# The first column pair of a feed-forward network: w1's combinations kept for the second half of the tokens

## The chip, the cores and the metric

The kernel runs on one core of a Trainium2 chip. The time is that of one execution on the device in microseconds (us); a median of three runs is given. TensorE (PE) does matmuls and transposes, VectorE (DVE) and GpSimd (POOL) do elementwise work on tiles in SBUF, ScalarE (ACT) does copies, casts and activations, and SyncE (SP) issues the DMAs. Each engine works through its own queue in order; semaphores make it wait for the others.

## What is computed

The reference is one layer of an encoder over 1024 tokens of 1024 channels. The part that matters here is the last but one line:

```python
h = _layer_norm(DEEPNORM_ALPHA * h + y @ w_out[l], ln1_g[l], ln1_b[l])
f = (jax.nn.silu(h @ ffn_w1[l]) * (h @ ffn_w3[l])) @ ffn_w2[l]
h = _layer_norm(DEEPNORM_ALPHA * h + f, ln2_g[l], ln2_b[l])
```

`ffn_w1` and `ffn_w3` are 1024 x 2816, `ffn_w2` is 2816 x 1024, all in float32.

## The kernel before

Products of float32 matrices are made of three matmuls each: every operand is split into a high part (a cast on ScalarE, L1384) and a low part (a subtraction, L1385, on POOL or on VectorE), and `mm3` (L160 to L162) adds high x high, high x low and low x high.

The feed-forward part multiplies blocks by a scheme of Strassen's kind: seven products of combined blocks in place of eight. Rows of w1 and w3 are halved over the 1024 input channels, columns over pairs of column tiles: pair p takes column tiles p and p + 11, p = 0 to 10. Tokens are halved into two *halves* h = 0, 1 of 256 columns each (a column stands for two tokens, one from each block). For each pair, w1 and then w3 give seven combined left operands, here called *pieces* 1 to 7 (`split` in `ff_stream`, tiles fc, hi and lo). The combinations are made by VectorE: L1575, L1576, L1579 and L1581. `H[h][i]` is the right operand of product i for half h. `ff_hidden` multiplies piece by piece into PSUM banks (fx, fz, fy), copies them out with ScalarE (L1633, L1639, L1642, L1644), adds on VectorE (L1636, L1645, L1648), applies silu (L1622) after w1 and multiplies by it after w3 (L1625). The four result blocks are then combined for the second matrix product (LEFT, seven left sides), split into high and low parts and written to HBM (`put_by`, tiles fg, L1658, L1385, L1661 into d_f).

All pairs but the first are done for both halves at once (512 columns). The first pair is done for half 0, then for half 1, and `ff_stream` loads, combines and splits w1 and w3 anew for the second half. Half 0 needs only the normalised tokens 512 to 1023 (`turn` 0 and 1), half 1 the rest. `turn` (L1507 to L1535) transposes two token tiles (ot on TensorE, hb copies L1519), scales and saves them (L1520, L1521, d_acc), combines them (L1528, L1529, L1532, L1535) and splits the seven combinations into H. `turn` 2 and 3 are called after `ff_stream` has been started and run beside the first products. What precedes them is the layer norm, whose last step is L1466.

Tiles live in named places (tags) that are handed round in rings: "w" raw weights (4), "s" sums (2), "c" pieces (6), "e" results (8), "g" left sides (2). A tile's new use waits until its old one is read. P0 to P5 and T5 held the token tiles (acc) before, T7, WR, WL and WH what `turn` 2 and 3 combine (hb), LA0, LA1, C1 and C2 the output weights.

The order on each engine is set by a scheduler at build time, from the order of the calls, priorities and its own estimate of times; nothing is reordered while the kernel runs.

Of the kernel before, what the change touches and what calls it, by code (L numbers as in the profile page):

```python
# [13 lines left out]
R = mybir.dt.float32r  # L14
I32 = mybir.dt.int32
AF = mybir.ActivationFunctionType
ALU = mybir.AluOpType
# [8 lines left out]
NF = FF // 128  # L26
# [113 lines left out]
class Trunk:  # L140
# [1407 lines left out]


    def ff_order(self):  # L1550
        return [(0, (0,)), (0, (1,))] + [(p, (0, 1)) for p in range(1, NF // 2)]


    def ff_stream(self):
        nc, A = self.nc, self.A
        tt = nc.vector.tensor_tensor
        self.rings = {"w": ["Z0", "Z1", "MW", "T6"], "s": ["P0", "P1"], "c": ["Z2", "P2", "LA0", "LA1", "C1", "C2"],
                      "e": ["P3", "P4", "P5", "T5", "T7", "WR", "WL", "WL"], "g": ["WH", "WH"]}
        self.banks = ["pj", "q", "fs", "q", "z", "pj", "q", "fs"]

        def split(x, eng=None):
            c = self.ring("c", [128, 2, 4, 128], R)
            self.split_to(c[:, 0], c[:, 1], x.rearrange("p (k n) -> p k n", k=4), eng)
            return c[:, 0], c[:, 1]
        for p, hs in self.ff_order():
            for nm in ("w1", "w3"):
                raw = [self.ring("w", [128, 2, 512]) for i in range(2)]
                for i in range(2):
                    nc.sync.dma_start(out=raw[i].rearrange("p a n -> p (a n)"), in_=A[nm][p + i * NF // 2])
                (a11, a12), (a21, a22) = ([x[:, i] for i in range(2)] for x in raw)  # L1570
                yield split(a11)
                yield split(a12)
                s = self.ring("s", [128, 2, 512])
                a5, a6 = s[:, 0], s[:, 1]
                tt(out=a5, in0=a21, in1=a22, op=ALU.add)  # L1575
                tt(out=a6, in0=a5, in1=a11, op=ALU.subtract)  # L1576
                yield split(a6, nc.vector)
                yield split(a5)
                tt(out=a21, in0=a11, in1=a21, op=ALU.subtract)  # L1579
                yield split(a21)  # L1580
                tt(out=a12, in0=a12, in1=a6, op=ALU.subtract)  # L1581
                yield split(a12, nc.vector)
                yield split(a22)

    def ff_next(self):
        if len(self.ahead) < 4:
# [7 lines left out]
        return x  # L1594


    def ff_hidden(self, p, hs):
        nc = self.nc
        tt = nc.vector.tensor_tensor
        n = 256 * len(hs)  # L1600
        cs = slice(256 * hs[0], 256 * hs[0] + n)


        def product(i, ps, first):
            hi, lo = self.ff_next()
            for a, h in enumerate(hs):
                x = self.H[h][i]
                for k in range(4):
                    self.mm3(ps[:, 256 * a:256 * a + 256], hi[:, k], lo[:, k], x[:, 0, :, k], x[:, 1, :, k],
                             first and a == 0 and k == 0, a == len(hs) - 1 and k == 3, True)  # L1610
        act = [None] * 4
        have, put = {}, set()
        for w in range(2):
            ea, eb = (self.ring("e", [128, 2, 512])[:, :, :n] for i in range(2))
            e1, e2, e3, e5 = ea[:, 0], ea[:, 1], eb[:, 0], eb[:, 1]
            if w == 0:
                ex = self.ring("e", [128, 2, 512])[:, :, :n]


            def done(i, dst, src):  # L1620
                if w == 0:
                    nc.scalar.activation(out=dst, in_=src, func=AF.Silu)  # L1622
                    act[i] = dst
                else:
                    tt(out=dst, in0=src, in1=act[i], op=ALU.mult)  # L1625
                    have[i] = dst
                    for m, (a, *b) in enumerate(LEFT):
                        if m not in put and all(j in have for j in (a, *b[:1])):
                            put.add(m)
                            self.put_by(m, p, cs, have[a], *((have[b[0]], b[1]) if b else ()))  # L1630
# [6 lines left out]
            done(0, e1, e1)  # L1637
# [8 lines left out]
            done(3, e3, e3)  # L1646
            product(5, y, False)
            tt(out=e2, in0=y, in1=e2, op=ALU.add)  # L1648
            done(1, e2, e2)
            product(6, x, False)  # L1650
            done(2, ex[:, w], x)


    def put_by(self, m, p, cs, x, y=None, op=None):
        nc = self.nc
        g = self.ring("g", [128, 2, 512])[:, :, :cs.stop - cs.start]
        if y is not None:
            nc.vector.tensor_tensor(out=g[:, 1], in0=x, in1=y, op=op)  # L1658
            x = g[:, 1]
        self.split_to(g[:, 0].bitcast(R), g[:, 1], x, nc.vector)  # L1660
        nc.sync.dma_start(out=self.d_f[m, p, :, :, cs], in_=g)  # L1661

# [160 lines left out]
            nc.sync.dma_start(out=out, in_=o)  # L1823

    def ffn(self):
        for p, hs in self.ff_order():
            self.ff_hidden(p, hs)
        self.ff_second()


# [11 lines left out]
```

## Time and profile before

| | us |
|---|---|
| median of 3 runs (lowest, highest) | 1462.27 (1462.12, 1463.15) |
| profiled execution, its own time | 1465.01 |
| its span, first to last instruction | 1462.2 |
| TensorE matmul busy | 1323.2 (90%) |
| VectorE busy | 1100.0 (75%) |
| ScalarE busy | 621.7 (43%) |
| POOL busy | 575.7 (39%) |
| mean granted clock of TensorE | 0.958 |

Times within the profile count from the start of the span. The feed-forward part begins at 774.65 us; its second product begins at about 1230 us. Matmuls are pipelined: one of 128x256 is listed with 0.28 us but the next starts some 0.12 us later, so progress is read from the starts, and "busy" is the time covered. A row of a timeline gives start, duration, engine, line, operation and tiles (out<-in), the count, and in brackets the idle time of the engine before it and what ended it. The granted clock is 1.00 at 2.4 GHz and 0.50 at 1.2 GHz.

### The profile page before, as it was taken

What the parts mean: (1) busy time and instruction counts of PE and PEld (TensorE: products, weight loads), DVE (VectorE), ACT (ScalarE), POOL (GpSimd) and SP (SyncE); (2) the same over time, 40 slices, a digit from 0 to 9 for tenths busy, and PEclk for the clock granted to TensorE, in tenths of its full rate; (3) what the DMA queues carried; (4) which work ended last, traced back from release to release, by engine and by line L of the source; (5) the groups of instructions that cost most, each with busy time, mean ns of one, the idle gap of its engine ahead of it and who ended that gap; (6) DMA issues with size and microseconds to landing.
All of it is one profiled execution on the core that took longest, in us unless ns stands there. A gap on an engine that the chain in (4) does not pass through costs nothing.

```text
span 1462.2 us, 23749 instructions
## 1 busy us (share of the span) xinstructions
PE 1323.2 (90%) x9072; PEld 1196.4 (82%) x9072; DVE 1100.0 (75%) x1910; ACT 621.7 (43%) x1205; POOL 575.7 (39%) x524
## 2 busy tenths in 40 slices
PE   6968797977797999999877899999999999999997
PEld 5968787766796787877766899999999999888885
DVE  8997966487997685779999866666676665346888
ACT  4312141656324785761426544444444444332231
POOL 6466663153574332325567633333333331000006
PEclk9989998999899898999999899999999999999999
DMA  6111033122325004244312434444444438996752
GB/s 241 49 54 29 13 94 87 44 70 89 87 73 180 2 15 148 84 128 154 118 70 87 138 123 159 147 147 143 157 147 142 150 137 291 385 315 234 273 188 115
DMA packets 97056, 193.95 MB, mean 133 GB/s; under 512 B 24624, under 2 KB 50864, under 8 KB 96944
## 3 DMA queue, kind: packets, MB, share of 16 engines
q1 hardware_dynamic: 94912, 187.59, 38.3%
q10 hardware_dynamic: 2032, 4.86, 1.0%
q8 instruction: 71, 1.16, 0.3%
q14 instruction: 41, 0.34, 0.1%
HBM read 127.41 MB, written 63.96 MB: 131 GB/s over the span
## 4 chain that ended last, share of the span: by engine, by line
PE 42%; DVE 12%; DMA 3%; issue 2%; ACT 1%; POOL 1%; DVEq 0%; SPq 0%; ACTq 0%; POOLq 0%
PE fx L160 5%; PE fx L162 5%; PE fx L161 5%; PE f L160 4%; PE f L162 4%; PE f L161 4%; PE fy L162 2%; PE fy L160 2%; PE fy L161 2%; DVE acc L1435 1%; PE fz L160 1%; PE fz L161 1%; PE fz L162 1%; DMA fw<-w 1%; PE ops L161 1%
## 5 line engine op out<-in xcount | busy, mean ns | idle before, releaser
L160 PE MATMUL proj<-HA,wh 128*128 128x256 f32 x672 | 195.5, 291 | 14.6 <-DVE la L919 11.8
L160 PE MATMUL fx<-H,fc 128*128 128x256 f32 x704 | 196.9, 284 | 5.7 <-ACT fc L1384 2.2
L161 PE MATMUL proj<-HB,wh 128*128 128x256 f32 x672 | 200.1, 298 | 1.7 <-POOL HB L334 1.7
L162 PE MATMUL proj<-HA,wl 128*128 128x256 f32 x672 | 196.6, 293 | 4.1 <-POOL wl L394 4.1
L162 PE MATMUL fx<-H,fc 128*128 128x256 f32 x704 | 197.8, 282 | 2.6 <-DVE fc L1385 2.6
L1385 POOL TENSOR_TENSOR fc<-fw,fc 128x512 fp32r<-128x512 f32 x96 | 137.3, 1432 | 158.5 <-ACT fc L1384 157.7
L161 PE MATMUL fx<-H,fc 128*128 128x256 f32 x704 | 198.5, 282 | 0.0
L160 PEld LDWEIGHTS proj<-HA,wh 128*128 128x128 f32 x672 | 131.8, 196 | 18.4 <-issue 7.7
L162 PEld LDWEIGHTS proj<-HA,wl 128*128 128x128 f32 x672 | 131.5, 196 | 10.0 <-issue 5.5
L160 PEld LDWEIGHTS fx<-H,fc 128*128 128x128 f32 x704 | 132.5, 190 | 7.8 <-ACT fe L1633 2.7
L161 PEld LDWEIGHTS proj<-HB,wh 128*128 128x128 f32 x672 | 131.5, 196 | 7.0 <-issue 4.8
L162 PEld LDWEIGHTS fx<-H,fc 128*128 128x128 f32 x704 | 133.7, 191 | 2.8 <-DVE fc L1385 2.8
L161 PEld LDWEIGHTS fx<-H,fc 128*128 128x128 f32 x704 | 134.1, 191 | 0.1
L160 PE MATMUL f<-fb,fa 128*128 128x512 f32 x276 | 108.9, 395 | 0.0
L162 PE MATMUL f<-fb,fa 128*128 128x512 f32 x276 | 108.9, 394 | 0.0
L161 PE MATMUL f<-fb,fa 128*128 128x512 f32 x276 | 108.7, 394 | 0.0
L160 PE MATMUL fy<-H,fc 128*128 128x256 f32 x352 | 100.0, 284 | 4.7 <-ACT fe L1642 3.6
L162 PE MATMUL fy<-H,fc 128*128 128x256 f32 x352 | 99.5, 284 | 0.2 <-DVE fc L1385 0.2
L161 PE MATMUL fy<-H,fc 128*128 128x256 f32 x352 | 99.5, 283 | 0.0
L1821 POOL TENSOR_TENSOR acc<-acc,g 128x1024 f32<-128x1024 f32 x4 | 11.6, 2904 | 205.8 <-ACT acc L1820 205.8
L1384 ACT CAST fc<-fw 128x512 fp32r<-128x512 f32 x120 | 73.7, 619 | 31.8 <-POOL fc L1385 15.7
L1385 POOL TENSOR_TENSOR fc<-fs,fc 128x512 fp32r<-128x512 f32 x24 | 33.4, 1391 | 119.4 <-ACT fc L1384 116.0
(602 smaller groups left out, 3761.6 us busy)
## 6 DMA issues: line engine op xcount, KB each, us to landing
fa<-d_f SPq DMA_DIRECT2D x77, 512.0 KB, 3.8
d_f<-fg SPq DMA_DIRECT2D x70, 512.0 KB, 2.9
fw<-w SPq DMA_DIRECT2D x48, 512.0 KB, 3.6
fg<-w SPq DMA_DIRECT2D x44, 256.0 KB, 5.3
wraw<-w_in SPq DMA_DIRECT2D x16, 512.0 KB, 4.0
xt<-x SPq DMA_DIRECT2D x8, 512.0 KB, 8.1
oraw<-w_out SPq DMA_DIRECT2D x8, 512.0 KB, 3.7
yraw<-d_y SPq DMA_DIRECT2D x8, 512.0 KB, 4.1
```

What stands on the lines that cost most here:

```text
L160: mm(out, whi, xhi, start=start, stop=False, skip_group_check=shared)
L161: mm(out, whi, xlo, start=False, stop=False, skip_group_check=shared)
L162: mm(out, wlo, xhi, start=False, stop=stop, skip_group_check=shared)
L1384: nc.scalar.copy(out=hi, in_=raw)
L1385: (eng or nc.gpsimd).tensor_tensor(out=lo, in0=raw, in1=hi.bitcast(F32), op=ALU.subtract)
L1435: nc.vector.tensor_tensor(out=ht, in0=ht, in1=self.row4[1], op=ALU.add)
L1821: nc.gpsimd.tensor_tensor(out=o, in0=o, in1=self.g2, op=ALU.mult)
```

## The change

The first pair is still done by halves, but in the order w1 half 0, w3 half 0, w1 half 1, w3 half 1, all within one call of `ff_hidden`. The seven pieces of w1 made for half 0 are kept in a ring of their own ("k": Z2, P2, P3, T7, WR, WH, WH; tiles fk) and used again for half 1. w3's pieces are made twice, as before. While the first pair lasts, pieces of w3 have four places (C1, C2, LA0, LA1) and results five (P4, P5, T5, WL, WL), allocated once at full width and written by halves. The left sides are put by once, after the second half, 512 wide, into the tiles of ring "k", which the second use of w1 has then released. After that the places of "k" go to rings "c", "e" and "g".

```diff
     def ff_order(self):
-        return [(0, (0,)), (0, (1,))] + [(p, (0, 1)) for p in range(1, NF // 2)]
+        split = [(w, (h,)) for h in range(2) for w in range(2)]
+        return [split] + [[(w, (0, 1)) for w in range(2)] for p in range(1, NF // 2)]
...
-        self.rings = {"w": ["Z0", "Z1", "MW", "T6"], "s": ["P0", "P1"], "c": ["Z2", "P2", "LA0", "LA1", "C1", "C2"],
-                      "e": ["P3", "P4", "P5", "T5", "T7", "WR", "WL", "WL"], "g": ["WH", "WH"]}
+        self.rings = {"w": ["Z0", "Z1", "MW", "T6"], "s": ["P0", "P1"], "c": ["C1", "C2", "LA0", "LA1"],
+                      "e": ["P4", "P5", "T5", "WL", "WL"], "g": [], "k": ["Z2", "P2", "P3", "T7", "WR", "WH", "WH"]}
...
-            c = self.ring("c", [128, 2, 4, 128], R)
+            c = self.ring(ring, [128, 2, 4, 128], R)
...
+        for p, steps in enumerate(self.ff_order()):
+            kept = []
+            for w, hs in steps:
+                if kept and w == 0:
+                    yield from kept
+                    continue
+                ring = "c" if len(hs) == 2 or w else "k"
+                for x in parts(("w1", "w3")[w], p):
+                    if ring == "k":
+                        kept.append(x)
+                    yield x
...
+        tiles = [[self.ring("e", [128, 2, 512]) for i in range(3 - w)] for w in range(2)]
+        for w, hs in steps:
+            n = 256 * len(hs)
+            cs = slice(256 * hs[0], 256 * hs[0] + n)
...
+                tt(out=dst, in0=src, in1=act[i, hs], op=ALU.mult)
+                if hs[-1] == 1:
+                    have[i] = all_
...
+                            self.put_by(m, p, have[a], *((have[b[0]], b[1]) if b else ()))
...
+        if p == 0:
+            k = self.rings["k"]
+            self.rings["c"] += k[:2]
+            self.rings["e"] += k[2:5]
+            self.rings["g"] += k[5:]
...
+    def put_by(self, m, p, x, y=None, op=None):
         nc = self.nc
-        g = self.ring("g", [128, 2, 512])[:, :, :cs.stop - cs.start]
+        g = self.ring("g" if self.rings["g"] else "k", [128, 2, 512])
...
-        nc.sync.dma_start(out=self.d_f[m, p, :, :, cs], in_=g)
+        nc.sync.dma_start(out=self.d_f[m, p], in_=g)
```

`parts(nm, p)` is the body that loads one matrix's raw tiles and yields its seven pieces, unchanged; lines move down by one to 17 (L1575 to L1576 and so on). The scheduler puts the engines' instructions into another order. VectorE, from the end of the last layer norm on, before (fs_705 and fw_699, fw_700 are the second half's w1, fc_688 the third piece of w3, H and hb belong to `turn` 3):

```order
L1575 TENSOR_TENSOR fs_705_7266<-fw_700_7220 128x512
L1385 TENSOR_TENSOR H_654_6918<-hb_664_6970,H_654_6918 128x512
L1576 TENSOR_TENSOR fs_705_7266<-fs_705_7266,fw_699_7219 128x512
L1579 TENSOR_TENSOR fw_700_7220<-fw_699_7219,fw_700_7220 128x512
L1528 TENSOR_TENSOR hb_666_6972<-hb_664_6970 128x512
L1581 TENSOR_TENSOR fw_683_7085<-fw_683_7085,fs_687_7123 128x512
L1529 TENSOR_TENSOR hb_666_6972<-hb_665_6971,hb_666_6972 128x512
L1532 TENSOR_TENSOR hb_664_6970<-hb_665_6971,hb_664_6970 128x512
L1535 TENSOR_TENSOR hb_665_6971<-hb_665_6971,hb_666_6972 128x512
L1385 TENSOR_TENSOR H_655_6919<-hb_666_6972,H_655_6919 128x512
L1645 TENSOR_TENSOR fe_672_7020<-fe_672_7020 128x256
L1385 TENSOR_TENSOR fc_688_7126<-fs_687_7123,fc_688_7126 128x512
```

The same place now (fk_682 is piece 6 of w1, fc_695 piece 6 of w3, fz_699 product 2 of w1 for half 1):

```order
L1385 TENSOR_TENSOR H_654_6918<-hb_664_6970,H_654_6918 128x512
L1385 TENSOR_TENSOR fc_695_7181<-fw_685_7087,fc_695_7181 128x512
L1648 TENSOR_TENSOR fe_671_7019<-fz_680_7047,fe_671_7019 128x256
L1648 TENSOR_TENSOR fe_674_7022<-fz_694_7179,fe_674_7022 128x256
L1528 TENSOR_TENSOR hb_666_6972<-hb_664_6970 128x512
L1529 TENSOR_TENSOR hb_666_6972<-hb_665_6971,hb_666_6972 128x512
L1532 TENSOR_TENSOR hb_664_6970<-hb_665_6971,hb_664_6970 128x512
L1535 TENSOR_TENSOR hb_665_6971<-hb_665_6971,hb_666_6972 128x512
L1636 TENSOR_TENSOR fe_674_7022<-fe_674_7022,fe_671_7019 128x256
L1648 TENSOR_TENSOR fe_671_7019<-fz_699_7284,fe_671_7019 128x256
L1385 TENSOR_TENSOR H_655_6919<-hb_666_6972,H_655_6919 128x512
L1385 TENSOR_TENSOR fk_682_7053<-fw_645_6843,fk_682_7053 128x512
```

The three combinations of the second half's w1 are gone, the fourth combination of w3 (L1581, now L1582) and the low part of its third piece stand further up, and the low part of w1's piece 6 has come in after the turn. POOL, over the same time, before:

```order
L1385 TENSOR_TENSOR H_654_6918<-hb_665_6971,H_654_6918 128x512
L1385 TENSOR_TENSOR fc_686_7105<-fw_683_7085,fc_686_7105 128x512
L1385 TENSOR_TENSOR H_656_6920<-hb_658_6922,H_656_6920 128x512 x2
L1385 TENSOR_TENSOR fc_697_7202<-fw_684_7086,fc_697_7202 128x512
L1385 TENSOR_TENSOR fc_689_7143<-fs_687_7123,fc_689_7143 128x512
L1385 TENSOR_TENSOR H_656_6920<-hb_665_6971,H_656_6920 128x512
L1385 TENSOR_TENSOR H_654_6918<-hb_666_6972,H_654_6918 128x512
L1385 TENSOR_TENSOR H_655_6919<-hb_664_6970,H_655_6919 128x512
L1385 TENSOR_TENSOR fc_701_7223<-fw_699_7219,fc_701_7223 128x512
L1385 TENSOR_TENSOR H_656_6920<-hb_665_6971,H_656_6920 128x512
```

And POOL now (fk_679, fk_681 and fk_683 are pieces 4, 5 and 7 of w1, fc_696 is piece 7 of w3):

```order
L1385 TENSOR_TENSOR H_654_6918<-hb_665_6971,H_654_6918 128x512
L1385 TENSOR_TENSOR H_656_6920<-hb_658_6922,H_656_6920 128x512 x2
L1385 TENSOR_TENSOR fk_679_7031<-fs_677_7025,fk_679_7031 128x512
L1385 TENSOR_TENSOR H_656_6920<-hb_665_6971,H_656_6920 128x512
L1385 TENSOR_TENSOR fc_696_7198<-fw_686_7088,fc_696_7198 128x512
L1385 TENSOR_TENSOR H_654_6918<-hb_666_6972,H_654_6918 128x512
L1385 TENSOR_TENSOR H_655_6919<-hb_664_6970,H_655_6919 128x512
L1385 TENSOR_TENSOR fk_681_7049<-fw_646_6844,fk_681_7049 128x512
L1385 TENSOR_TENSOR H_656_6920<-hb_665_6971,H_656_6920 128x512
L1385 TENSOR_TENSOR fk_683_7070<-fw_646_6844,fk_683_7070 128x512
```

Low parts of w3 and of the second half's w1 have made room for those of w1's pieces 4, 5 and 7. On SyncE, the loads now (fw_715 and fw_716 are w1 of the next pair, fw_701 and fw_702 w3 of the second half):

```order
L1570 DMA fw_715_7445<-w1 128x1024
L1521 DMA d_acc_95<-acc_641_6825 128x1024
L1570 DMA fw_716_7446<-w1 128x1024
L1570 DMA fw_701_7313<-w3 128x1024
L1570 DMA fw_702_7314<-w3 128x1024
L1570 DMA fw_739_7643<-w3 128x1024
L1678 DMA d_f_96<-fk_712_7424 128x1024
```

The loads of the second half's w1 are gone, and w1 of the next pair is asked for ahead of w3 of the second half.

## Rows read from the trace of the kernel before

**Rows 1.** Stretches of the span: the stretch and its length, busy time of each engine with its count of instructions, TensorE's granted clock, the busy share of the DMA engines, GB/s.

```profile
774.65:790.00 15.35, 11.20 (x78) 10.34 (x77) 15.21 (x19) 12.60 (x23) 11.84 (x8) 0.89 0.51 172
790.00:806.07 16.07, 9.43 (x71) 8.33 (x69) 16.07 (x12) 10.46 (x21) 14.79 (x10) 0.91 0.08 33
...
860.00:880.00 20.00, 20.00 (x172) 20.00 (x171) 12.87 (x15) 8.56 (x16) 8.00 (x7) 1.00 0.27 90
880.00:900.00 20.00, 20.00 (x171) 19.99 (x170) 14.68 (x20) 10.03 (x18) 6.68 (x6) 1.00 0.60 212
```

The columns after the length are PE, PEld (weight loads), DVE, ACT and POOL.

**Rows 2.** TensorE in order of time, from the first matmul of the feed-forward part to the last wait of its start; the last row groups the transposes up to 806 us (busy time, mean ns, idle before).

```profile
774.65 0.36 PE L160 MATMUL fx<-H,fc 128*128 128x256 f32 x1
...
806.07 0.58 PE L162 MATMUL fx<-H,fc 128*128 128x256 f32 x1 [2.56 <-DVE fc L1385]
806.45 0.41 PE L160 MATMUL fx<-H,fc 128*128 128x256 f32 x1
806.66 0.41 PE L161 MATMUL fx<-H,fc 128*128 128x256 f32 x1
...
834.37 0.58 PE L160 MATMUL fy<-H,fc 128*128 128x256 f32 x1 [2.58 <-ACT fe L1642]
834.75 0.41 PE L161 MATMUL fy<-H,fc 128*128 128x256 f32 x1
834.96 0.41 PE L162 MATMUL fy<-H,fc 128*128 128x256 f32 x1
...
851.13 0.39 PE L160 MATMUL fx<-H,fc 128*128 128x256 f32 x1 [0.87 <-ACT fe L1639]
...
L1518 PE MATMUL ot<-ident,acc 128*128 128x128 f32 x23 | 3.4, 276 | 2.1 <-DVE acc L1466 1.8 <-ACT hb L1519 0.3
```

**Rows 3.** Whom TensorE waited for from 774.6 to 851.3 us: us in total, times, longest.

```profile
PE fy L160 <- ACT fe L1642: 3.6, 2, 2.6
PE fx L162 <- DVE fc L1385: 2.6, 1, 2.6
PE fx L160 <- ACT fc L1384: 2.2, 2, 1.4
PE fx L160 <- ACT fe L1633: 2.1, 3, 1.3
```

**Rows 4.** VectorE in order of time from the last step of the last layer norm to the low part of the third piece of w3.

```profile
785.87 2.30 DVE L1466 SCALAR_TENSOR_TENSOR acc<-acc,bnr,rows 128x1024 f32<-128x1024 f32 x1
...
788.42 1.44 DVE L1575 TENSOR_TENSOR fs<-fw 128x512 f32<-128x512 f32 x1
789.78 1.78 DVE L1385 TENSOR_TENSOR H<-hb,H 128x512 fp32r<-128x512 f32 x1
791.49 1.76 DVE L1576 TENSOR_TENSOR fs<-fs,fw 128x512 f32<-128x512 f32 x1
793.17 1.79 DVE L1579 TENSOR_TENSOR fw<-fw,fw 128x512 f32<-128x512 f32 x1
...
804.27 1.75 DVE L1385 TENSOR_TENSOR fc<-fs,fc 128x512 fp32r<-128x512 f32 x1
```

**Rows 5.** POOL: two rows in order of time (the last one ends `turn` 3), and its low parts of pieces over the whole span, grouped.

```profile
790.98 3.43 POOL L1385 TENSOR_TENSOR H<-hb,H 128x512 fp32r<-128x512 f32 x2
...
805.43 1.72 POOL L1385 TENSOR_TENSOR H<-hb,H 128x512 fp32r<-128x512 f32 x1
...
L1385 POOL TENSOR_TENSOR fc<-fw,fc 128x512 fp32r<-128x512 f32 x96 | 137.3, 1432 | 158.5 <-ACT fc L1384 157.7
```

**Rows 6.** VectorE: five rows in order of time (the second half's w1 in the first three, then the same operation for later tiles, beside POOL at 817.02 us and without it at 825.33 us); the operations of putting by from 804 to 839 us, all of the first half's; and the same at full width from 880 to 1120 us (count, busy time, mean ns, idle before).

```profile
809.05 0.68 DVE L1385 TENSOR_TENSOR fc<-fs,fc 128x512 fp32r<-128x512 f32 x1
...
811.90 1.77 DVE L1581 TENSOR_TENSOR fw<-fw,fs 128x512 f32<-128x512 f32 x1
...
817.02 1.78 DVE L1575 TENSOR_TENSOR fs<-fw 128x512 f32<-128x512 f32 x1
...
823.30 0.68 DVE L1385 TENSOR_TENSOR fc<-fw,fc 128x512 fp32r<-128x512 f32 x1
...
825.33 0.68 DVE L1575 TENSOR_TENSOR fs<-fw 128x512 f32<-128x512 f32 x1
...
L1385 DVE TENSOR_TENSOR fg<-fg 128x256 f32<-128x256 f32 x5 | 3.1, 635 | 0.5 <-ACT fg L1384 0.5
L1658 DVE TENSOR_TENSOR fg<-fe,fe 128x256 f32<-128x256 f32 x4 | 2.4, 607 | 1.6 <-DMA d_f<-fg 1.6
L1385 DVE TENSOR_TENSOR fg<-fe,fg 128x256 f32<-128x256 f32 x2 | 1.9, 963 | 0.0
L1658 DVE TENSOR_TENSOR fg<-fe 128x256 f32<-128x256 f32 x1 | 1.5, 1509 | 0.0
...
L1385 DVE TENSOR_TENSOR fg<-fg 128x512 f32<-128x512 f32 x31 | 21.2, 685 | 1.6
L1658 DVE TENSOR_TENSOR fg<-fe,fe 128x512 f32<-128x512 f32 x24 | 18.3, 761 | 13.2 <-DMA d_f<-fg 13.0
```

**Rows 7.** ScalarE's casts of pieces from 774 to 851 us, grouped as above.

```profile
L1384 ACT CAST fc<-fw 128x512 fp32r<-128x512 f32 x23 | 13.9, 619 | 1.9 <-PE fy L162 1.5 <-PE fz L162 0.4
```

**Rows 8.** DMAs issued from 770 to 851 us: tiles, count, size, median us from issue to landing.

```profile
fw<-w SPq DMA_DIRECT2D x10, 512.0 KB, 3.8
d_acc<-acc SPq DMA_DIRECT2D x4, 512.0 KB, 3.0
```

More of the change, by code (lines that the diff above doesn't have):

```diff
@@ L1561, in split @@
         def split(x, eng=None):
-            c = self.ring("c", [128, 2, 4, 128], R)
+            c = self.ring(ring, [128, 2, 4, 128], R)
             self.split_to(c[:, 0], c[:, 1], x.rearrange("p (k n) -> p k n", k=4), eng)
             return c[:, 0], c[:, 1]
[L1565 to L1583, printed above, removed]
@@ new lines, in parts @@
+        def parts(nm, p):
+            raw = [self.ring("w", [128, 2, 512]) for i in range(2)]
+            for i in range(2):
+                nc.sync.dma_start(out=raw[i].rearrange("p a n -> p (a n)"), in_=A[nm][p + i * NF // 2])
+            (a11, a12), (a21, a22) = ([x[:, i] for i in range(2)] for x in raw)
+            yield split(a11)
+            yield split(a12)
+            s = self.ring("s", [128, 2, 512])
+            a5, a6 = s[:, 0], s[:, 1]
+            tt(out=a5, in0=a21, in1=a22, op=ALU.add)
+            tt(out=a6, in0=a5, in1=a11, op=ALU.subtract)
+            yield split(a6, nc.vector)
+            yield split(a5)
+            tt(out=a21, in0=a11, in1=a21, op=ALU.subtract)
+            yield split(a21)
+            tt(out=a12, in0=a12, in1=a6, op=ALU.subtract)
+            yield split(a12, nc.vector)
+            yield split(a22)
@@ L1594, in ff_next, with ff_hidden, product, done @@
         return x
-    def ff_hidden(self, p, hs):
+    def ff_hidden(self, p, steps):
         nc = self.nc
         tt = nc.vector.tensor_tensor
[L1600 to L1614, printed above, removed]
+        act, have, put = {}, {}, set()
+        tiles = [[self.ring("e", [128, 2, 512]) for i in range(3 - w)] for w in range(2)]
+        for w, hs in steps:
+            n = 256 * len(hs)
+            cs = slice(256 * hs[0], 256 * hs[0] + n)
+            def product(i, ps, first):
+                hi, lo = self.ff_next()
+                for a, h in enumerate(hs):
+                    x = self.H[h][i]
+                    for k in range(4):
+                        self.mm3(ps[:, 256 * a:256 * a + 256], hi[:, k], lo[:, k], x[:, 0, :, k], x[:, 1, :, k],
+                                 first and a == 0 and k == 0, a == len(hs) - 1 and k == 3, True)
+            ea, eb, ex = *(x[:, :, cs] for x in tiles[w][:2]), tiles[0][2][:, :, cs]
             e1, e2, e3, e5 = ea[:, 0], ea[:, 1], eb[:, 0], eb[:, 1]
-            if w == 0:
-                ex = self.ring("e", [128, 2, 512])[:, :, :n]
-            def done(i, dst, src):
+            whole = lambda t, i: tiles[t][i // 2][:, i % 2]
+            def done(i, dst, src, all_):
                 if w == 0:
                     nc.scalar.activation(out=dst, in_=src, func=AF.Silu)
[L1623 to L1626, printed above, removed]
+                    act[i, hs] = dst
+                    return
+                tt(out=dst, in0=src, in1=act[i, hs], op=ALU.mult)
+                if hs[-1] == 1:
+                    have[i] = all_
                     for m, (a, *b) in enumerate(LEFT):
@@ L1629, in done @@
                             put.add(m)
-                            self.put_by(m, p, cs, have[a], *((have[b[0]], b[1]) if b else ()))
+                            self.put_by(m, p, have[a], *((have[b[0]], b[1]) if b else ()))
             x = self.bank([128, 512], "fx")[:, :n]
@@ L1636, in ff_hidden @@
             tt(out=e1, in0=z, in1=e1, op=ALU.add)
-            done(0, e1, e1)
+            done(0, e1, e1, whole(w, 0))
             product(2, x, False)
@@ L1645, in ff_hidden @@
             tt(out=e3, in0=e3, in1=e5, op=ALU.add)
-            done(3, e3, e3)
+            done(3, e3, e3, whole(w, 2))
             product(5, y, False)
             tt(out=e2, in0=y, in1=e2, op=ALU.add)
-            done(1, e2, e2)
+            done(1, e2, e2, whole(w, 1))
             product(6, x, False)
-            done(2, ex[:, w], x)
-    def put_by(self, m, p, cs, x, y=None, op=None):
+            done(2, ex[:, w], x, tiles[0][2][:, 1])
+        if p == 0:
[4 more added lines that the diff above has]
+    def put_by(self, m, p, x, y=None, op=None):
         nc = self.nc
-        g = self.ring("g", [128, 2, 512])[:, :, :cs.stop - cs.start]
+        g = self.ring("g" if self.rings["g"] else "k", [128, 2, 512])
         if y is not None:
@@ L1825, in ffn @@
     def ffn(self):
-        for p, hs in self.ff_order():
-            self.ff_hidden(p, hs)
+        for p, steps in enumerate(self.ff_order()):
+            self.ff_hidden(p, steps)
         self.ff_second()
```

## Prediction

> **What bounds the kernel now.** I read the page first: TensorE is busy for 90% of the span and is the largest share of the chain. The table of stretches then shows where it is not [rows 1]. From 860 us on it starts 171 or 172 matmuls in every 20 us, one per 0.1163 us, at a granted clock of 1.00; nothing that another engine saves there can shorten the time. The loss lies at the start of the feed-forward part. Its first matmul starts at 774.65 us and the last wait of the start-up ends at 851.13 us [rows 2]. In order of program 434 matmuls of 128x256 lie between: 124 before the one at 806.07 us, 310 from there to 851.13 us. At full rate 434 take 50.5 us; 76.5 us went by. The transposes among them (ot) are busy for 3.4 us [rows 2], so 22.6 us are lost: 13.6 of them before 806.07 us and 45.06 - 310 x 0.1163 = 9.0 after it.
>
> The list of who waited for whom [rows 3] puts TensorE's waits down to ScalarE and VectorE: copies out of PSUM (L1633, L1642, L1639), casts (L1384) and low parts (L1385). These stand in queues: VectorE is busy for all 16.07 us from 790 to 806.07 us and POOL for 14.79 [rows 1]. What fills VectorE is a mix of the layer's turn (L1528 to L1535, H), the combinations for the next w1 (L1575 to L1581) and the left sides put by (fg) [rows 4, 6]. The longest single wait of that stretch, 2.56 us to 806.07 us, is for the low part of fc_688, which stands on VectorE behind three combinations of the second half's w1 [rows 2, 4]. TensorE also pays for having waited: after 2.56 us and after 2.58 us of waiting matmuls start 0.21 us apart, half the granted clock, where others start 0.12 us apart [rows 1, 2].
>
> **The change part by part.** *Removed.* Seven splits of the second half's w1: on VectorE 1.44 + 1.76 + 1.79 us [rows 4] and 1.77 + 0.68 + 0.68 us [rows 6], 8.1 us in all; on POOL five low parts of 1.43 us, 7.2 us [rows 5]; on ScalarE seven casts of 0.62 us, 4.3 us [rows 7]; two loads of 512 KB.
>
> *Moved and merged.* The first half's twelve VectorE operations of putting by (8.9 us between 809 and 838 us) [rows 6] go. The second half's become 512 wide, 0.69 and 0.76 us each [rows 6], so 24 narrow ones turn into 12 wide ones of some 8.7 us together. At the first half's price the 24 take 17.8 us, at half of a wide operation's time each 8.7; so between none and 9.1 us of VectorE's work go. I count none, as the first half's operations were slow beside POOL. What is left comes later, partly under the next column pair. VectorE is busy for 12.87 and 14.68 us of 20 in full flow [rows 1], which covers it once TensorE has caught up. If that cover is gone, the copies out of PSUM wait behind it; I count that below.
>
> *New waits.* Pieces 3 to 7 of the first w1 no longer go to tiles that are free at 772 us, but to P3, T7, WR, WH, WH, which the turn of the last four token tiles reads to its end. The next tiles for results (P4 instead of P3) wait for the saved copy of token tile 2, a DMA of 3.0 us [rows 8] issued some 3 us later than the one of token tile 3, by about 783 us; it lands near 786, before its first use at 789, and costs nothing. If that cover is gone, each microsecond is one for TensorE. The last two raw tiles of w3 reuse those of w1 and so wait for pieces 6 and 7.
>
> *Until piece 6.* In the new order VectorE does two more 512-wide operations before L1466 of token tile 0 and one fewer. So L1466 ends near 790 instead of 788.17 us [rows 4]. TensorE has 60 matmuls to do before it and is through near 783 us; it waits for almost 7 us. Before, it had done 62 matmuls at 790.5 us, with its waits in pieces: even. Then VectorE's low part of H (1.7 us) frees it at 791.7. POOL's queue from there is two H, fk_679, H, fc_696, H, six of some 1.7 us [rows 5], to 802.3 us; TensorE meets that point after some 3 us of waiting in all. Piece 6 needs a cast (0.62) and a low part of 1.7 us more: 804.7 us. By then 148 matmuls are done, where before 124 were at 806.07 us. Term 1: 1.4 us earlier and 24 x 0.1163 = 2.8 us more work, 4.2 us.
>
> *From there to full rate.* I followed the queues with the same durations. TensorE waits about 0.7 us for VectorE, which has three combinations of the next pair in front; 0.3 to 1.8 us for a copy behind the cast of fc_706; 0.9 to 2.4 us for the copy two casts on; 0.3 us at piece 5 of w3; and 0.7 to 2.3 us at 842 to 847 us, where a silu waits behind the wide put-by operations. Together 2.9 to 7.5 us against 9.0 now. The lower ends take 0.68 us for a 512-wide VectorE operation, as at 825.33 us, the upper ones 1.7, as at 817.02 us, where POOL was running [rows 6]. Term 2: 1.5 to 6.1 us. The sum is 5.7 to 10.3 us.
>
> VectorE's 817.02 us row took 1.78 us beside a POOL operation and the 825.33 us row, with POOL idle, 0.68 [rows 6]. The Trainium skill, SBUF — State Buffer, section "Who interferes with whom", says that a VectorE instruction with two SBUF inputs and a GpSimd one that reads SBUF exclude each other for the whole instruction. By that rule five POOL operations fewer give VectorE about their length back, and the sum would be at its upper end.
>
> I take the lower end, because queues followed by hand lose time only at the waits that I see. After the long wait to 790 us and one more, matmuls start 0.095 us later each (0.21 less 0.117), for 12 of them 1.1 us. Some of that is in the stretch before too; I take off 0.7. The gain is 5.0 us. The profiled execution took 1465.01 us, 2.8 more than its span of 1462.2, and stands 2.7 above the median; a profile of the changed kernel should show some 1460.0, and the timed median 1462.27 - 5.0 = 1457.3 us.
>
> **The rivals.**
> *Nothing to be measured.* POOL's queue behind L1466 ends the turn at 807.15 us before and at about the same time after, as the operations that leave it are replaced by fk_679, fk_681 and fk_683 [rows 5]. If TensorE hangs on POOL there, term 1 is the 24 matmuls less what the half clock takes. For it speaks that POOL is busy for 14.79 of 16.07 us [rows 1]; against it that the wait to 806.07 us is for VectorE alone. With one more half-clock stretch of 1.1 us at each of three waits and the upper waits of term 2, the gain is 5.7 - 3.3 - 1 = 1.4 us: 1460.9 us. The Trainium skill, TensorE: Matmul & The Clock Gate, section "Part 1: The HAM clock gate", says that the throttled clock is the default and that activity releases it; the trace agrees where the two waits above end at half clock. By that rule the change's one long wait is worse than several short ones of the same sum, which is this rival's mechanism.
>
> *Much better.* The put-by operations and the combinations leave VectorE so free that no wait is left after 804.7 us. Then 4.2 + 9.0, less 1, are won: 1450.1 us. Against it: the 12 wide operations and the next pair's combinations meet near 840 us.
>
> *Slower.* The last two raw tiles of w3 are late. Their load waits for piece 7, which waits for POOL's last H at 807.15 us: cast 0.62, POOL 1.43, load 3.8 [rows 7, 5, 8], 813.0 us; three combinations and a low part of 0.68 to 1.7 us each and a cast put fc_706 at 816 to 821 us. TensorE wants it near 820. Each microsecond later is one lost, and ScalarE and VectorE hold everything else behind these waits, as they work in order. From about 830 us on the gain is gone; at 835, which the SP queue (fw_715 and fw_716 stand in front) would have to cause, the time is 1467 us. Against it: fw_716 waits only for fc_696, near 800 us.
>
> *It doesn't do what it says*: the second half would split w1 again. The order shows no second set; I give it nothing.
>
> **How the numbers follow.** The forecast, a gain of 3 to 8 us, has 0.52 (1454.3 to 1459.3); much better 0.13; nothing 0.25; slower 0.10. A difference under 0.2%, 2.9 us, can't be told from none here. So faster has 0.65, same 0.25, slower 0.10. The range of 1452.0 to 1463.0 us takes in the sum's upper end and the second case and leaves out half of the better and the slower case.
>
> **What would show it.** The profile should show no second set of fs for w1, TensorE waiting once for some 7 us for L1466 near 790 us, no wait for a low part at 806 us, and 148 matmuls by about 805 us. Full rate should come near 847 us or before, at a matmul that now starts at 853. The 12 wide fk operations should lie between 822 and 841 us. I am wrong if TensorE waits for more than 8 us in all after 805 us, or if a cast of fc_703 or fc_706 waits for a load.

## The result and the profile after

| | before | after |
|---|---|---|
| median of 4 runs (lowest, highest), us | 1462.19 (1461.71, 1463.15) | 1451.72 (1450.45, 1452.14) |
| span of the profiled execution | 1462.2 | 1450.0 |
| its first matmul of the feed-forward part | 774.65 | 774.05 |
| VectorE, POOL, ScalarE busy | 1100.0, 575.7, 621.7 | 1082.1, 571.9, 616.1 |

The ratio is 0.9926, with a 95% interval of 0.9909 to 0.9943: faster by 10.5 us, twice the forecast 5.0 and just outside the stated range. A second measurement (`c1_changed_again` below) gave 0.9915 (0.9901 to 0.9929). The ratios in this document leave out one execution, of the kernel called e2b below, that took 2539.6 us where its others took 1461 to 1467.

Where did it come from? The same stretches as in [rows 1], now of the changed kernel (PE, PEld, DVE, ACT, POOL busy with counts; granted clock, DMA share, GB/s):

```profile
774.65:790.00 15.35, 12.86 (x95) 12.26 (x94) 15.28 (x21) 13.27 (x25) 11.11 (x8) 0.89 0.28 106
790.00:806.07 16.07, 13.41 (x110) 12.80 (x109) 14.09 (x12) 9.44 (x20) 15.34 (x10) 1.00 0.39 129
806.07:834.37 28.30, 27.67 (x233) 27.26 (x232) 21.29 (x30) 13.20 (x30) 14.57 (x11) 1.00 0.27 93
...
860.00:880.00 20.00, 20.00 (x171) 20.00 (x170) 18.16 (x22) 9.07 (x17) 7.88 (x6) 1.00 0.41 150
```

Up to 806 us TensorE starts 205 matmuls and transposes where it started 149, and 233 instead of 190 to 834 us. From 860 us on the rate is what it was. POOL is as busy as before from 790 to 806 us; VectorE has two microseconds free. The granted clock is 1.00 where [rows 1] has 0.91.

Whom TensorE waited for from 774 to 851 us (total, times, longest), to be set against [rows 3]:

```profile
PE fx L160 <- ACT fe L1651: 1.9, 2, 1.7
PE fx L161 <- POOL H L1385: 1.6, 1, 1.6
PE fx L160 <- ACT H L1384: 1.4, 1, 1.4
PE ot L1518 <- DVE acc L1466: 1.1, 1, 1.1
PE fy L162 <- POOL fk L1385: 1.0, 1, 1.0
PE fy L160 <- DVE fe L1660: 0.4, 1, 0.4
```

The casts and low parts of pieces (L1384, L1385 into fc) are gone from the list. What is left is the turn of the last four token tiles (H, L1466) up to 800 us, one low part of a kept piece (fk, 1.0 us), an addition (L1660, 0.4) and one late copy (L1651). TensorE in order of time, at the places that the terms of the sum speak of:

```profile
774.05 0.36 PE L160 MATMUL fx<-H,fk 128*128 128x256 f32 x1
...
785.52 1.76 PE L1518 MATMUL ot<-ident,acc 128*128 128x128 f32 x8 [1.14 <-DVE acc L1466]
...
801.65 0.39 PE L162 MATMUL fy<-H,fk 128*128 128x256 f32 x1
...
840.60 0.38 PE L160 MATMUL fx<-H,fc 128*128 128x256 f32 x1 [1.67 <-ACT fe L1651]
...
869.92 0.29 PE L161 MATMUL fz<-H,fc 128*128 128x256 f32 x1
```

The row at 801.65 us begins after 148 matmuls of the feed-forward part, the last one after 700. The matmul after 700 in the kernel before is this row of its trace:

```profile
882.65 0.28 PE L161 MATMUL fz<-H,fc 128*128 128x256 f32 x1
```

That gives one measure for all kernels below, the *loss*: the time from the first of these matmuls to the one after n, less n x 0.1163 us (the transposes count as lost too). After 700 it is 882.65 - 774.65 - 81.4 = 26.6 us before and 869.92 - 774.05 - 81.4 = 14.5 us after: 12.1 us less.

| loss in us after n matmuls | 60 | 124 | 148 | 200 | 300 | 434 | 500 | 700 |
|---|---|---|---|---|---|---|---|---|
| before | 9.0 | 17.0 | 19.2 | 19.8 | 20.5 | 26.0 | 26.3 | 26.6 |
| after | 3.0 | 8.3 | 10.4 | 11.3 | 11.8 | 12.1 | 14.2 | 14.5 |

Three short waits for copies after 860 us come to 1.2 us, where the kernel before has one of 0.4. The loss says more here than the whole time: the first matmul of the part lay anywhere from 769 to 775 us in the profiles of kernels with the same code ahead of it, while the changed kernel, profiled twice, lost 14.5 and 14.4 us. What follows hardly differs: from the matmul after 700 to the end of the span every kernel profiled here takes 578.5 to 580.2 us, but for e2 with 601.8. So two spans differ by where the part starts and by its loss, and the 12.1 us of loss and the 10.5 us between the medians agree within the spread of the starts.

### The profile page after: what moved, and what is told of

Read it like the earlier page. It is cut to its first block, busy times and chain, and to the rows that moved or that the text cites. A ratio compares the mean times of both kernels' runs of the same rounds, so it can differ in the third digit from the quotient of the medians.

```text
span 1450.0 us, 23654 instructions
## 1 busy us (share of the span) xinstructions
PE 1315.7 (91%) x9072; PEld 1190.8 (82%) x9072; DVE 1082.1 (75%) x1892; ACT 616.1 (42%) x1191; POOL 571.9 (39%) x519
## 4 chain that ended last, share of the span: by engine, by line
PE 40%; DVE 11%; DMA 4%; POOL 3%; issue 2%; ACT 1%; DVEq 0%; SPq 0%; ACTq 0%; POOLq 0%
PE f L160 4%; PE f L162 4%; PE f L161 4%; PE fx L160 4%; PE fx L162 4%; PE fx L161 4%; DMA fw<-w 2%; PE fy L160 2%; PE fy L162 2%; PE fy L161 2%; DVE acc L1435 1%; POOL H L1385 1%; PE fz L161 1%; PE fz L160 1%; PE fz L162 1%
## 5 line engine op out<-in xcount | busy, mean ns | idle before, releaser
L1385 POOL TENSOR_TENSOR fc<-fw,fc 128x512 fp32r<-128x512 f32 x88 | 126.4, 1439 | 162.1 <-ACT fc L1384 161.3
L160 PE MATMUL fx<-H,fc 128*128 128x256 f32 x672 | 186.6, 282 | 3.1 <-ACT fe L1651 1.9
L161 PE MATMUL fx<-H,fc 128*128 128x256 f32 x672 | 188.6, 281 | 0.0
L162 PE MATMUL fx<-H,fc 128*128 128x256 f32 x672 | 188.1, 280 | 0.0
L162 PEld LDWEIGHTS proj<-HA,wl 128*128 128x128 f32 x672 | 130.5, 194 | 10.3 <-issue 5.5
L160 PEld LDWEIGHTS fx<-H,fc 128*128 128x128 f32 x672 | 125.5, 189 | 4.2 <-ACT fe L1651 2.3
L161 PEld LDWEIGHTS fx<-H,fc 128*128 128x128 f32 x672 | 126.9, 189 | 0.1
L162 PEld LDWEIGHTS fx<-H,fc 128*128 128x128 f32 x672 | 126.7, 189 | 0.0
L162 PE MATMUL fy<-H,fc 128*128 128x256 f32 x336 | 94.6, 282 | 0.0
L160 PE MATMUL fy<-H,fc 128*128 128x256 f32 x336 | 94.5, 281 | 0.0
L161 PE MATMUL fy<-H,fc 128*128 128x256 f32 x336 | 94.4, 281 | 0.0
L1384 ACT CAST fc<-fw 128x512 fp32r<-128x512 f32 x110 | 67.7, 618 | 30.7 <-POOL fc L1385 13.9
L1385 POOL TENSOR_TENSOR fc<-fs,fc 128x512 fp32r<-128x512 f32 x22 | 30.2, 1372 | 109.3 <-ACT fc L1384 101.6
```

What stands on the lines that cost most here:

```text
L160: mm(out, whi, xhi, start=start, stop=False, skip_group_check=shared)
L161: mm(out, whi, xlo, start=False, stop=False, skip_group_check=shared)
L162: mm(out, wlo, xhi, start=False, stop=stop, skip_group_check=shared)
L1385: (eng or nc.gpsimd).tensor_tensor(out=lo, in0=raw, in1=hi.bitcast(F32), op=ALU.subtract)
```

## The experiments

The theories. *Work*: the gain is the removed splits of the second half's w1, on VectorE or on POOL. *Put-by*: it comes from putting the left sides by once. *Contention*: it is larger than the sum because VectorE's operations are short where POOL stands still.

| kernel | ratio to before (95%) | loss after 700, us |
|---|---|---|
| changed kernel, again (c1) | 0.9915 (0.9901 to 0.9929) | 14.4 |
| e1, put by per half | 0.9924 (0.9908 to 0.9939) | 18.7 |
| e2, merge only | 1.0129 (1.0114 to 1.0144) | 25.0 |
| e2b, merge only, ring turned | 1.0010 (0.9999 to 1.0021) | 29.0 |
| e3, POOL's gap filled | 0.9913 (0.9898 to 0.9927) | 16.2 |
| e5p, POOL's work back | 0.9955 (0.9939 to 0.9970) | 22.6 |
| e5v, VectorE's work back | 0.9963 (0.9949 to 0.9978) | 21.1 |
| e7, turn's low parts on VectorE | 0.9869 (0.9854 to 0.9884) | 11.2 |
| e8, and those of the pieces | 0.9889 (0.9876 to 0.9903) | 12.0 |
| e9, e7's edit on the kernel before | 0.9990 (0.9981 to 0.9999) | 25.8 |
| e10, e7 for all eight token tiles | 0.9866 (0.9852 to 0.9879) | 13.2 |
| e11, memsets on POOL | one run, 1453.52 us beside 1462.44 | 15.5 |

In e8 two and in e10 eight matmuls of the part run 12 and 7 us ahead of the others, among the products before it. The loss of these two counts from the first fx after them and leaves them out; with them it is 11.8 and 12.3 us.

**Keeping against merging.** The first run keeps the pieces and undoes the merge:

```diff
-                if hs[-1] == 1:
-                    have[i] = all_
+                have[i, hs] = dst
...
-                            self.put_by(m, p, have[a], *((have[b[0]], b[1]) if b else ()))
+                        self.put_by(m, p, cs, have[a, hs], *((have[b[0], hs], b[1]) if b else ()))
```

> The pieces of w1 kept, but the left sides put by per half, 24 operations of 256 columns, in an eighth of H's space that is free (combined left sides of the first pair are rounded to the matmul's format on the way, so that part of the output is less exact). If keeping the pieces is what counts, nearly all of the gain stays: 1451 to 1454 us. If putting by once is what counts, VectorE has twelve narrow operations more between 800 and 838 us, as the kernel before had, and copies out of PSUM wait behind them: 1455 to 1458 us.

The second merges and doesn't keep, with the rings of the kernel before:

```diff
...
-                if kept and w == 0:
-                    yield from kept
-                    continue
-                ring = "c" if len(hs) == 2 or w else "k"
...
+                ring = "c"
+                yield from parts(("w1", "w3")[w], p)
...
```

> The order by halves within one pair and the left sides put by once, 512 wide, but w1 split again for the second half, with the rings of the kernel before. If the removed splits count (8.1 us on VectorE, 7.2 on POOL), the gain is mostly gone: 1458 to 1463 us. If putting by once counts, most of it stays: 1453 to 1457 us.

e1 keeps the gain as far as times can tell (1453.1 us, as expected if keeping is what counts). In its trace it loses 18.7 us, 4.2 more than the changed kernel: 6.8 from the 200th to the 350th matmul, where the changed kernel loses 0.8, and 1.9 less after that. The largest wait there: VectorE stops for a left side's DMA, ScalarE's cast of a left side waits for VectorE, and the copy that TensorE needs stands behind both (rows of VectorE, ScalarE and TensorE, in e1; H stands for the space that holds the left sides):

```profile
819.72 0.43 DVE L1679 TENSOR_TENSOR H<-fe,fe 128x256 fp32r<-128x256 f32 x1 [0.94 <-DMA d_f<-H]
...
821.83 0.41 ACT L1384 CAST H<-H 128x256 fp32r<-128x256 f32 x1 [1.20 <-DVE H L1679]
...
823.07 0.58 PE L160 MATMUL fx<-H,fc 128*128 128x256 f32 x1 [3.02 <-ACT fe L1651]
```

So the merged put-by is worth some 4 us in the profiles once the pieces are kept. How much of that is its width isn't shown, since e1's left sides also have only two places of their own, and the wait for the DMA is for one of them; the changed kernel has the seven of ring "k". The times (0.9924 beside 0.9926 and 0.9915) neither show nor exclude the 4 us.

e2 came out slower than any theory had it: 18.9 us more than before. Its loss at the start is 25.0 us, like before's. The rest is one wait at the start of the second product, and the half clock around its end (the first row is from the list of waits, the second one a stretch with the columns of [rows 1]; the kernel before has a clock of 1.00 there):

```profile
PE f L160 <- DMA fa<-d_f: 19.0, 1, 19.0
...
1240.00:1260.00 20.00, 7.16 (x20) 5.69 (x21) 5.45 (x8) 3.09 (x5) 0.00 (x0) 0.54 0.63 218
```

The first pair turns the ring of results by five places now instead of ten, so the second product's first tiles, which inherit those places, may lie where the last pair still works. The next run turns the ring by five once more:

```diff
+        if p == 0:
+            e = self.rings["e"]
+            e[:] = e[5:] + e[:5]
```

> As e2_merge_only, but with ring e turned by five places after the first pair, so that the second product's first tiles lie where they lay in the kernel before. If the 19 us wait for a tile of the second product came from the place of that tile, it is gone, and what is left is what merging is worth without keeping: by the loss in the feed-forward part of e2 (25.0 against 26.6 us) 1 to 3 us less than before: 1459 to 1462 us. If merged put-by itself delays the second product's loads, the wait stays: 1478 to 1484 us.

The 19 us are gone. The 1 to 3 us that I expected on top didn't come: merging without keeping is worth nothing (1.0010; its loss is 2.4 us more than before's). The put-by theory falls as the cause of the gain; the gain hangs on the kept pieces.

**Which engine's work.** The changed kernel, with work that nothing reads added where the second use of w1 begins, on one engine at a time, beside the changed kernel itself:

> The changed kernel once more, beside the runs below on the same chip. Its feed-forward part should lose the same 14 to 15 us of TensorE's time up to its 700th matmul as in the first profile, whatever the stages ahead of it take; 1450 to 1453 us, a ratio of 0.991 to 0.994.

```diff
+                    for i, x in enumerate(kept):
+                        if i not in (2, 5):
+                            nc.gpsimd.tensor_tensor(out=self.y1[:, i % 2, :4], in0=x[0].bitcast(F32), in1=x[1].bitcast(F32), op=ALU.subtract)
+                        yield x
```

> The changed kernel with five subtractions of 128x512 on POOL in the place of the five low parts that it no longer makes (they read the kept pieces and write space that nothing reads). If POOL's work makes VectorE's operations long and POOL's queue holds H back, a third or more of the gain goes: the loss up to the 700th matmul rises from 14.5 to 17 us or more, 1454 to 1458 us. If only VectorE's own work counted, POOL's can be there or not: under 1 us, 1450 to 1453 us.

e5v does the same with 3, 1 and 2 subtractions on VectorE ahead of the third, fifth and sixth piece.

> The changed kernel with six subtractions of 128x512 on VectorE in the place of the four combinations and two low parts that it no longer makes. If VectorE's queue is what copies and casts waited behind, 6 x 0.68 to 6 x 1.7 = 4 to 10 us of work come back to it before the second use of w1, and the loss rises by 3 to 7 us: 1454 to 1459 us. If POOL alone counted, under 1 us.

Work on either engine costs: POOL's five bring 8.1 us of loss back, VectorE's six 6.6, and the medians are 5.9 and 7.6 us above the changed kernel's 1450.67. They don't price the removed splits, though, and the two sizes can't be added up. In both kernels the added work stands ahead of the layer norm's last step (L1466), which ends 17.9 (e5p) and 18.0 us (e5v) after the part's first matmul; it is 11.3 us in the changed kernel and 13.5 in the kernel before. Nor did any run put back the seven casts on ScalarE and the two loads that went with the splits, so their share of the gain isn't shown. Whom TensorE waited for longest, in e5p (first row) and in e5v:

```profile
PE fx L161 <- DVE H L1385: 3.8, 1, 3.8
```

```profile
PE fx L161 <- DVE H L1385: 5.5, 1, 5.5
PE fy L160 <- DVE fe L1663: 2.9, 1, 2.9
```

In both it is H that is late, VectorE's low part of it, even where all the added work is POOL's. In e5p the layer norm's L1465, which takes 1.27 us in the changed kernel and in e5v, stands beside POOL's work:

```profile
776.57 2.32 DVE L1465 SCALAR_TENSOR_TENSOR acc<-acc,bnmv,rows 128x1024 f32<-128x1024 f32 x1
```

**Contention.** e3 computes one low part of H three times, at a place where POOL was idle. One VectorE operation of that stretch moves down by two rows; nothing else is reordered on any engine:

```diff
         put(1, b21, nc.gpsimd)
+        if j == 2:
+            for i in range(2):
+                nc.gpsimd.tensor_tensor(out=H[1][:, 1, 0], in0=b21, in1=H[1][:, 0, 0].bitcast(F32), op=ALU.subtract)
```

> The changed kernel with one low part on POOL (product 2 of the second half, token tile pair 2) computed three times instead of once, so that POOL has work between 778.2 and 782.5 us, where it was idle. If VectorE's operations before the last step of token tile 0's layer norm were short (0.68 us) because POOL was idle, four or five of them take 1.2 to 1.8 us again, that step ends 2 to 4 us later than 785.4, and the time is 1453.5 to 1456 us. If POOL's work doesn't matter to VectorE there, only two POOL operations are added in a gap: 785.4 us as now and 1451 to 1452.5 us.

The changed kernel first: POOL, then VectorE from the layer norm's L1465 to its last step.

```profile
776.51 1.71 POOL L1385 TENSOR_TENSOR H<-hb,H 128x512 fp32r<-128x512 f32 x1
782.47 1.82 POOL L1385 TENSOR_TENSOR H<-hb,H 128x512 fp32r<-128x512 f32 x1 [4.24 <-ACT H L1384]
...
778.70 1.27 DVE L1465 SCALAR_TENSOR_TENSOR acc<-acc,bnmv,rows 128x1024 f32<-128x1024 f32 x1
...
779.97 0.67 DVE L1385 TENSOR_TENSOR H<-hb,H 128x512 fp32r<-128x512 f32 x1
780.56 0.68 DVE L1529 TENSOR_TENSOR hb<-hb,hb 128x512 f32<-128x512 f32 x1
...
783.58 1.80 DVE L1466 SCALAR_TENSOR_TENSOR acc<-acc,bnr,rows 128x1024 f32<-128x1024 f32 x1
```

And e3, whose feed-forward part starts at 769.25 us, 4.8 earlier:

```profile
773.51 3.86 POOL L1530 TENSOR_TENSOR H<-hb,H 128x512 fp32r<-128x512 f32 x2
...
773.90 2.31 DVE L1465 SCALAR_TENSOR_TENSOR acc<-acc,bnmv,rows 128x1024 f32<-128x1024 f32 x1
...
776.21 1.71 DVE L1385 TENSOR_TENSOR H<-hb,H 128x512 fp32r<-128x512 f32 x1
...
781.69 2.05 DVE L1466 SCALAR_TENSOR_TENSOR acc<-acc,bnr,rows 128x1024 f32<-128x1024 f32 x1
```

Beside POOL the same operations take 2.31 and 1.71 instead of 1.27 and 0.67 us. The layer norm's last step ends 14.5 us after the part's first matmul instead of 11.3, and the loss is 2.0 us higher by the 148th matmul and 1.7 after 700. The time didn't show it (0.9913): 1.7 us is less than the spread of the starts. My expectation was right about the step's end; but three operations before it became longer, not four or five, and it was too sure about the time.

Is it any work of POOL? e11 asks for memsets there, which write SBUF and read nothing:

> The changed kernel with two memsets of 128x1024 on POOL where e3_pool_gap_filled had two subtractions: POOL is busy in the gap, but reads nothing. If what slows VectorE is POOL's reading of SBUF, VectorE's operations beside the memsets take their 0.68 us (1.27 for the 128x1024 step L1465) as in the changed kernel; if any POOL work slows it, they take 1.2 to 2.3 us as in e3. The scheduler orders some later work otherwise, so the whole time (1450 to 1456 us) says little; the rows are what counts.

The scheduler put the memsets earlier than e3's subtractions, 0.7 us after the part's first matmul (774.70 us), and a subtraction behind them. In e11:

```profile
775.42 1.84 POOL L1530 MEMSET H<- 128x1024 f32 x2
777.23 1.82 POOL L1385 TENSOR_TENSOR fc<-fw,fc 128x512 fp32r<-128x512 f32 x1
...
776.55 0.67 DVE L1585 TENSOR_TENSOR fw<-fw,fs 128x512 f32<-128x512 f32 x1
...
777.82 2.32 DVE L1465 SCALAR_TENSOR_TENSOR acc<-acc,bnmv,rows 128x1024 f32<-128x1024 f32 x1
...
780.13 1.70 DVE L1385 TENSOR_TENSOR H<-hb,H 128x512 fp32r<-128x512 f32 x1
```

In the changed kernel the first of these VectorE operations overlaps a subtraction of POOL:

```profile
775.90 1.18 DVE L1582 TENSOR_TENSOR fw<-fw,fs 128x512 f32<-128x512 f32 x1
```

Beside the memsets this combination with two inputs in SBUF takes 0.67 us. When POOL subtracts again, one operation still passes in 0.63 us (L1531, at 777.26 us), and the next two take 2.32 and 1.70. It is one row beside the memsets, L1465 didn't fall there, and e11 is a single run; but it points to POOL's reading. The Trainium skill, SBUF — State Buffer, section "Who interferes with whom", says just that: a VectorE instruction with two SBUF inputs contends with a GpSimd one that reads SBUF, not with one that only writes it. These rows agree.

**A better version.** If POOL's subtractions cost VectorE a microsecond each, VectorE may as well do them:

```diff
-            self.split_to(H[i][:, 0, j % 2], H[i][:, 1, j % 2], x, eng)
+            self.split_to(H[i][:, 0, j % 2], H[i][:, 1, j % 2], x, nc.vector if j > 1 else eng)
```

> The changed kernel with all low parts of H of the last four token tiles on VectorE, so that ten fewer POOL operations run from 776 to 804 us. If POOL's work is what makes VectorE's operations 1.7 instead of 0.68 us there, VectorE pays 6.8 us for the ten and gets about 1 us back on each of some ten others; H is complete earlier than 804.5 us: 1447 to 1451.5 us. If VectorE's queue is what it is by its count of operations, it has ten more in a stretch where it is busy for 14 of 16 us, H comes later and the time is 1455 to 1460 us.

It beats both kernels: 1444.75 us, 0.9869. VectorE and POOL from 790 to 806 us (the columns of [rows 1]), and the longest waits of TensorE up to 860 us:

```profile
790.00:806.00 16.00, 14.17 (x119) 13.73 (x118) 13.10 (x21) 11.41 (x23) 4.67 (x3) 1.00 0.31 106
```

```profile
PE fx L161 <- DVE H L1385: 3.3, 2, 2.2
PE fx L160 <- ACT fe L1651: 1.8, 3, 0.8
```

VectorE does 21 operations in 13.10 us where the changed kernel did 12 in 14.09. POOL's queue is also shorter by ten operations, so part of the gain can be that H no longer waits there; the two aren't separated.

> As e7_turn_low_on_dve, and the low parts of the first pair's pieces (w1 and both sets of w3) on VectorE too, 15 more operations there and POOL idle through the start of the feed-forward part. If POOL's use is what makes VectorE slow, each costs 0.68 us and the rest gains: the loss up to the 700th matmul falls from e7's 11.2 to 8 to 10.5 us, 1442 to 1446 us. If VectorE is now the bound by its own count, 15 x 0.68 = 10 us more stand in its queue and pieces come later: the loss rises to 12 to 16 us, 1447 to 1452 us.

e8 moves the low parts of the first pair's pieces as well. Its loss is 12.0 us, not below e7's 11.2, so the hoped-for 8 to 10.5 didn't come. That VectorE's own count is now the bound fits up to 790 us, where it is busy for 16.2 of 16.9 us; from 790 to 806 it is busy for only 12.4 of 16.0, so what bounds e8 there stays open. But e8 has the clearest rows on contention. POOL is idle until

```profile
818.85 1.29 POOL L1385 TENSOR_TENSOR fc<-fw,fc 128x512 fp32r<-128x512 f32 x1 [66.49 <-ACT fc L1384]
```

and all 50 additions and subtractions of 128x512 on VectorE from 770 to 818 us take 0.67 to 0.69 us. In the changed kernel 15 of its 27 in that time take 1.1 to 1.8 us; each of these overlaps a subtraction of POOL, and none of the seven that overlap none takes more than 0.69.

> The kernel before (w1 split again for the second half, left sides per half) with only the low parts of H of the last four token tiles moved from POOL to VectorE. If the two engines' holding each other up was the larger part of its loss of 26.6 us, it loses 18 to 23 us and takes 1455 to 1459 us without any work removed. If VectorE's queue was full by its own work, ten more operations make it worse: 1462 to 1468 us.

A miss too, and a telling one. The kernel before with e7's edit loses 6.5 us less by the 148th matmul (12.7 against 19.2), so H is early there as well. But it then loses 8.4 up to the 300th, where the kernel before loses 1.3, waiting for pieces (e9, from 768 to 860 us, the longest waits):

```profile
PE fx L160 <- ACT fc L1384: 3.6, 2, 2.8
PE fx L162 <- DVE fc L1385: 3.4, 1, 3.4
PE fz L162 <- POOL fc L1385: 2.5, 1, 2.5
```

With w1 split anew, the pieces are what TensorE waits for behind H; with w1 kept (e7's list above) they are not.

> As e7_turn_low_on_dve, and the low parts of H of token tiles 4 to 7 on VectorE too. They are made from 650 to 775 us, where VectorE is busy for 33.9 of 34.6 us beside POOL. If POOL's work costs VectorE a microsecond each there as well, the feed-forward part starts 2 to 5 us earlier than e7's 773.9: 1440 to 1445 us. If VectorE is bound by its own work there, ten more operations of 0.68 us delay the layer norms by up to 6.8 us: 1445 to 1452 us.

e10's first fx starts at 766.97 us, 7.0 before e7's, with eight matmuls done ahead of it, but it loses 2.0 us more (1.1 with the eight counted), and the time is e7's within the intervals: medians of 1443.94 and 1444.75 us. The profiles flatter the difference, as e10's is of its fastest execution and e7's of its slowest. What the earlier stage wins can't be told from this.

## Why the prediction was wrong

The mechanism held: no second set of splits, fewer waits, the same rate from 860 us on. The time was 5.6 us below the forecast, since both terms of the sum were too small.

- **Term 1, until piece 6.** Forecast 4.2 us, measured 17.0 - 10.4 = 6.6. The step that failed is "L1466 ends near 790": it ended at 785.4. I had counted operations more and fewer and priced each at its duration in [rows 4], 1.4 to 1.8 us, though the list for POOL had changed: its two low parts of 3.92 us beside that stretch had moved ahead, and it stood still for 4.24 us. TensorE waited 2.5 us there (1.4 and 1.1 in its list), not almost 7. With the gap filled (e3) the loss at the 148th matmul is 12.3 us; the forecast implies 12.8. Here I had one value with no bounds, so not even the sum's upper end held the result.
- **Term 2, to full rate.** Bounds 1.5 to 6.1 us, taken 1.5; measured 9.3 - 3.8 = 5.5, from the 124th matmul before and the 148th after, up to the 500th. This choice of the lower end is the largest error, 4.0 us. The copies behind fc_706's cast, for which I had 1.2 to 4.2 us, cost 0.26; the first three combinations ahead ran while POOL was idle. VectorE, and POOL's next operation, in the changed kernel:

```profile
811.35 0.68 DVE L1576 TENSOR_TENSOR fs<-fw 128x512 f32<-128x512 f32 x1
812.07 0.69 DVE L1577 TENSOR_TENSOR fs<-fs,fw 128x512 f32<-128x512 f32 x1
812.67 0.69 DVE L1580 TENSOR_TENSOR fw<-fw,fw 128x512 f32<-128x512 f32 x1
813.28 1.78 DVE L1582 TENSOR_TENSOR fw<-fw,fs 128x512 f32<-128x512 f32 x1
...
812.76 1.75 POOL L1385 TENSOR_TENSOR fc<-fs,fc 128x512 fp32r<-128x512 f32 x1 [1.62 <-DVE fs L1577]
```

- **The choice between the prices.** The prediction had the pair, 0.68 and 1.78 us, and cited the rule of the Trainium skill (SBUF — State Buffer, section "Who interferes with whom") that decides between them. It said that by that rule the sum is at its upper end, and then took the lower one because waits that the hand count doesn't see would eat the rest; it had no row for them. The loss fell by 12.1 us, more than the upper end of 10.3.
- **The half clock.** I took 0.7 us off for a long wait. Up to the matmul after 700, the trace before has 39 steps of 0.21 to 0.22 us from one matmul to the next, 3.8 us above full rate, in three stretches that begin at about 783, 806 and 835 us; the trace after has 7, 0.7 us, in one stretch behind L1466, and its second profile 14, 1.4 us. So 2.4 to 3.1 us of the gain, contained in the two terms, come from the clock, where I had a loss. The rival that one long wait is worse had the wrong premise, as the wait wasn't long.
- **Put by wide, late.** Right in place: the wide operations ran from 820 to 842 us, and the copy behind a silu cost 1.67 us at 840.60, within 0.7 to 2.3. That none of VectorE's work goes with the merging was too careful: its busy time fell by 17.9 us, of which the removed splits account for 8.1 by the prediction's count (of the five rows in time order in [rows 6], the second half's w1 is the first, second and fourth). How the other 9.8 divide between fewer operations and shorter ones isn't shown.
- **The rivals.** The late raw tiles of w3 (slower) didn't come: in the list of waits from 770 to 850 us no cast of a piece on ScalarE waits for a load. "Much better" at 1450.1 us had 0.13 and was the nearest. Of my own signs, TensorE waited 2.3 us after 805 us up to 851, not more than 8, full rate came at 840.6, before 847, and the 148 matmuls were done by 801.65, before 805; the one wait of some 7 us near 790 didn't come.

What stays open: how the gain divides between VectorE's splits, POOL's and ScalarE's casts; how much of the time, not of the trace, the merged put-by is worth; and how e10's earlier start and larger loss add up.

## What to carry to other kernels

Price an operation by what runs beside it in the new order, not by its row in the old one: here the same subtraction costs 0.68 or 1.7 us, so removing or shifting a neighbour's work can be worth as much as removing the engine's own. Before giving elementwise work to the second engine, compare its price there plus what it adds to the first one's operations. A part of a change that is worth nothing alone (the merge) can be worth something behind another, and a ring that turns by another count can cost more than the change brings.

## What the runs showed that I had not expected

- Both engines pay for the overlap: VectorE's 128x1024 step went from 1.27 to 2.31 us and a 128x512 one from 0.67 to 1.71, and POOL's subtractions in e3 took 1.93 us each, where POOL has rows of 1.30 us alone.
- Moving ten subtractions to an engine that was busy for 14 of 16 us from 790 to 806 us left that engine less busy there (13.10 us of 16.00) and the kernel 6 to 7 us faster than the changed one, by the medians.
- The feed-forward part of kernels with the same code ahead of it started at 769.25 to 774.97 us from one profiled execution to the next, though the loss after that came out within 0.1 us in the kernel that was profiled twice. A time alone hides effects of 2 us here.
